# A rebuilt opening: packed small inputs, a moved silu, and filler matmuls on zeros, in a two-layer transformer kernel

## The chip, the cores and the metric

The kernel runs on one core of one Trainium2 chip. The metric is the device time of one execution in microseconds; the time before is 995.08 us, the median of 3 runs (993.34 to 995.79). Names of engines: PE is TensorE's matmul, PEld its weight load, DVE is VectorE, ACT is ScalarE, POOL is GpSimd, SP is SyncE, which only issues transfers here.

## The reference, cut to what matters

Two layers, 256 tokens, width 1024. Each layer has a feed-forward block, a mixer (sliding-window attention in layer 0, forgetting attention in layer 1) and a second feed-forward block. Every block is preceded by a modulated norm, whose shift, scale and gate come from the condition vector c.

```python
c_act = jax.nn.silu(c)
for layer in range(DEPTH):
    mod = (c_act @ ada_w[layer] + ada_b[layer]).reshape(B, 3, 3, D_MODEL)
    h = modulate(x, norm_g[layer, 0], mod[:, 0, 0], mod[:, 0, 1])
    x = x + 0.5 * mod[:, 0, 2][:, None, :] * swiglu(h, ffn_w13[layer, 0], ffn_w2[layer, 0])
    h = modulate(x, norm_g[layer, 1], mod[:, 1, 0], mod[:, 1, 1])
    ...
# modulate: rmsnorm(x, g) * (1 + scale) + shift
# swiglu:   gate, up = split(h @ w13); (silu(gate) * up) @ w2
```

All in float32, about 250 MB of weights read once.

## The kernel before

**A recorded program, then a list scheduler.** Everything in `_build` is only recorded: `Recorder.add` (line 185) notes each instruction with its tiles and an assumed duration, and `Recorder.run` (line 309) then plays the whole program against a model of the engines and emits the instructions in the order that comes out. PE takes its matmuls in the order of their place in the program (`at`), every other engine the ready instruction with the earliest due time, where `urgent` overrides the due time. Each engine afterwards executes its own list strictly in order. A different opening therefore shifts the model's clock, and can exchange neighbours far behind it. Nearly every instruction has line 238 in the profile, the line that emits it, so groups are told apart by their tiles.

**Precision by three matmuls.** A weight piece of 128 x 1024 float32 (512 KB) lands in `wraw`; ACT casts it to `whi`, DVE makes `wlo` = raw - hi; `mm3` multiplies hi by hi, hi by lo and lo by hi. Raw, hi, lo, activations (`hT`) and some others share one pool of 39 slots (tag "w").

**Modulation on DVE.** The rows of ada_w are not multiplied on PE. silu(c) is broadcast over 128 partitions as `cb`, and each piece of ada_w costs one DVE instruction over 1024 columns, a "dot" (SCALAR_TENSOR_TENSOR wraw<-wraw,cb), with the sum in one column of `mod`.

**The opening** (lines 504 to 552, `start` at 712). SP loads c (one row), x (two pieces), then by turns two pieces of ada and two of w13 (`w13s`). ACT's queue loads `colb` and `gcol`; POOL's queue loads `qkg`, `sink` and `bfb`, which are first used in later layers. ACT takes silu of c on one partition, PE broadcasts it with a row of ones, ACT copies it to `cb`. x is normalised (squares with a sum on ACT, `u` on DVE, the power -1/2 on POOL, `xn`), PE transposes it against `ident` and ACT copies the transposes to `xT`. Then come eight steps over k: two dots give column k of shift and scale, ACT makes h, `hT` hi and lo follow, and PE does 24 matmuls into eight accumulators ("pa" and "ps"), the first four chunks of the first feed-forward block. Afterwards these are gated (`sil`), transposed by PE and evacuated by ACT and DVE (`gT`), while ACT and DVE go on splitting weight pieces (w13a, w2).

**Later places that matter.** At about 70 us PE transposes `sil` of these first chunks and needs banks that the evacuation of `gT` frees; at about 188 us, the end of the first block, it needs the last `sil`, which stands in DVE's list among dots for the modulation of later blocks.

## Time and profile before

| what | before |
|---|---|
| median of 3 runs | 995.08 us (993.34 to 995.79) |
| the profiled execution | 994.5 us, span 992.7 us |
| PE busy | 972.6 us (98%), 4766 matmuls |
| DVE busy | 776.9 us (78%) |
| ACT busy | 528.2 us (53%) |
| transfers | 252.73 MB, mean 255 GB/s |

How to read it: the span goes from the first instruction to the last end; the execution's time is 1.8 us longer. A row of the timeline gives start, duration, engine, line, operation, tiles and shapes, and in brackets the idle time of the engine just before and what ended it. A row of the waits gives who waited for whom, the total in us, how often, and the longest. Windows give the busy time of each engine in a stretch, the granted clock, the busy share of the DMA engines and GB/s.

### The profile page before, as it was taken

What the parts mean: (1) busy time and instruction counts of PE and PEld (TensorE: products, weight loads), DVE (VectorE), ACT (ScalarE), POOL (GpSimd) and SP (SyncE); (2) the same over time, 40 slices, a digit from 0 to 9 for tenths busy, and PEclk for the clock granted to TensorE, in tenths of its full rate; (3) what the DMA queues carried; (4) which work ended last, traced back from release to release, by engine and by line L of the source; (5) the groups of instructions that cost most, each with busy time, mean ns of one, the idle gap of its engine ahead of it and who ended that gap; (6) DMA issues with size and microseconds to landing.
All of it is one profiled execution on the core that took longest, in us unless ns stands there. A gap on an engine that the chain in (4) does not pass through costs nothing.

```text
span 992.7 us, 13662 instructions
## 1 busy us (share of the span) xinstructions
PE 972.6 (98%) x4766; PEld 816.3 (82%) x4766; DVE 776.9 (78%) x1396; ACT 528.2 (53%) x946; POOL 48.2 (5%) x73
## 2 busy tenths in 40 slices
PE   6999999999999999999999999999999999999998
PEld 4878788798888888888888888889899888888886
DVE  5999989985899988767898788658788998554622
ACT  6583434465986454444554453437677776444420
POOL 1000000012100000000100000001221010000000
PEclk9999999999999999999999999999999999999999
DMA  9999999856347987776788879744437458656501
GB/s 338 409 390 383 402 361 409 307 172 215 129 156 252 337 334 285 291 294 233 275 317 304 312 279 352 247 157 161 139 112 266 161 197 282 224 198 220 211 8 64
DMA packets 74247, 252.73 MB, mean 255 GB/s; under 512 B 8497, under 2 KB 11969, under 8 KB 74178
## 3 DMA queue, kind: packets, MB, share of 16 engines
q1 hardware_dynamic: 73186, 249.63, 68.6%
q10 hardware_dynamic: 896, 2.21, 0.6%
q8 instruction: 37, 0.61, 0.2%
q0 software_dynamic: 96, 0.02, 0.2%
q14 instruction: 32, 0.26, 0.1%
HBM read 249.95 MB, written 1.88 MB: 254 GB/s over the span
## 4 chain that ended last, share of the span: by engine, by line
PE 91%; DVE 4%; ACT 2%; DMA 2%; issue 1%; POOL 0%; SPq 0%; DVEq 0%; POOLq 0%
PE ps L238 57%; PE pa L238 34%; DVE wraw L238 1%; DVE wlo L238 1%; DMA wraw<-in_w13s 1%; DMA M<-foxsc 1%; ACT t L238 1%; POOL qrs L238 0%; ACT PT L238 0%; DVE t L238 0%; DVE gT L238 0%; DVE sil L238 0%; ACT whi L238 0%; SPq L238 0%; DVE qss L238 0%
## 5 line engine op out<-in xcount | busy, mean ns | idle before, releaser
L238 PE MATMUL ps<-whi,hT 128*128 128x512 f32 (+2 forms) x1728 | 534.8, 382 | 0.0
L238 ACT CAST whi<-wraw 128x1024 fp32r<-128x1024 f32 (+2 forms) x328 | 329.5, 1024 | 218.6 <-DMA wraw<-in_w 72.4
L238 DVE TENSOR_TENSOR wlo<-wraw,whi 128x1024 fp32r<-128x1024 f32 (+2 forms) x328 | 381.3, 1180 | 67.0 <-ACT whi L238 49.2
L238 PEld LDWEIGHTS ps<-whi,hT 128*128 128x128 f32 x1728 | 321.5, 188 | 52.9 <-issue 0.6
L238 PE MATMUL ps<-wlo,hT 128*128 128x512 f32 (+2 forms) x864 | 328.1, 381 | 0.0
L238 PE MATMUL pa<-whi,gT 128*128 128x512 f32 x704 | 218.0, 391 | 0.0
L238 DVE SCALAR_TENSOR_TENSOR wraw<-wraw,cb 128x1024 f32<-128x1024 f32 x144 | 173.3, 1218 | 15.5 <-DMA wraw<-in_ada 15.1
L238 PEld LDWEIGHTS ps<-wlo,hT 128*128 128x128 f32 x864 | 162.4, 188 | 26.1 <-issue 0.2
L238 PEld LDWEIGHTS pa<-whi,gT 128*128 128x128 f32 x704 | 131.9, 188 | 27.2
L238 PE MATMUL pa<-wlo,gT 128*128 128x512 f32 x352 | 133.3, 390 | 0.0
L238 ACT ACTIVATE sil<-ps 128x256 f32<-128x256 f32 x84 | 32.0, 384 | 105.6 <-PE ps L238 105.4
L238 PEld LDWEIGHTS pa<-wlo,gT 128*128 128x128 f32 x352 | 66.1, 188 | 13.6
L238 DVE TENSOR_TENSOR sil<-sil,ps 128x256 f32<-128x256 f32 x84 | 34.6, 414 | 48.2 <-ACT sil L238 48.1
L238 DVE TENSOR_TENSOR gT<-ps,gT 128x256 fp32r<-128x256 f32 x88 | 33.5, 415 | 8.9 <-ACT gT L238 8.9
L238 PE MATMUL pa<-whi,OT 128*128 128x512 f32 x128 | 39.1, 393 | 0.0
L238 PE MATMUL pa<-PT,zeroed 128*128 128x256 f32 (+1 forms) x192 | 36.3, 287 | 0.5 <-DVE PT L238 0.4
L238 ACT ACTIVATE t<-x 128x512 f32<-128x512 f32 x24 | 15.0, 625 | 40.8 <-DVE x L238 38.9
L238 DVE SCALAR_TENSOR_TENSOR t<-gate,pa 128x512 f32<-128x512 f32 (+1 forms) x26 | 15.6, 640 | 25.6 <-DMA gate<-gsc 12.9
L238 ACT CAST gT<-ps 128x256 fp32r<-128x256 f32 x88 | 29.1, 378 | 12.2 <-PE ps L238 11.6
L238 PEld LDWEIGHTS pa<-PT,zeroed 128*128 128x128 f32 x192 | 30.1, 191 | 3.8 <-DVE PT L238 1.2
L238 POOL TENSOR_TENSOR qrs<-qss,mhalf 128x4 f32<-128x4 f32 (+1 forms) x24 | 26.8, 1118 | 87.3 <-DVE qss L238 86.3
L238 PE MATMUL ps<-ident,sil 128*128 128x128 f32 x176 | 27.9, 272 | 2.6 <-DVE sil L238 1.4
(113 smaller groups left out, 650.7 us busy)
## 6 DMA issues: line engine op xcount, KB each, us to landing
wraw<-in_ada SPq DMA_DIRECT2D x144, 512.0 KB, 7.5
wraw<-in_w13b SPq DMA_DIRECT2D x132, 512.0 KB, 6.3
wraw<-in_w SPq DMA_DIRECT2D x88, 512.0 KB, 5.6
wraw<-in_w13a SPq DMA_DIRECT2D x28, 512.0 KB, 10.2
wraw<-in_fwin SPq DMA_DIRECT2D x28, 384.0 KB, 3.8
wraw<-in_w13s SPq DMA_DIRECT2D x16, 512.0 KB, 10.2
wraw<-in_swin SPq DMA_DIRECT2D x16, 384.0 KB, 5.2
wraw<-in_swout SPq DMA_DIRECT2D x8, 512.0 KB, 3.7
```

What stands on the lines that cost most here:

```text
L238: return lambda: getattr(real, method)(*[un(v) for v in a], **{n: un(v) for n, v in k.items()})
```

## The change

Five small inputs become one array of 232 columns that one transfer on ACT's queue brings; qkg, sink and bfb are now slices of it, and POOL issues no transfers. silu moves from the row of c to the copies after the broadcast; a silu of one column (`tb`) comes first on ACT, so that the table load is at the start. 21 matmuls of 128 x 512 on a zeroed tile `wz` are recorded as fillers: the model gives one to PE whenever nothing else is ready for it there, and they end up at fixed places in PE's list. Their results are never read. Three of the four squares of the first norm go to DVE (the model may choose, by `also`), all four `xn` run on DVE, and h in `start` is fixed on ACT. The second half of x's transposes (`transposed_x(1)`) stands behind the first chunk of the first step.

```diff
+NWARM = 21
...
-        pes = sorted((o for o in ops if o.eng == "PE"), key=lambda o: o.at)
+        pes = sorted((o for o in ops if o.eng == "PE" and not o.filler), key=lambda o: o.at)
+        fillers = [o for o in ops if o.filler]
...
+                    if pick is None and e == "PE" and fillers and fillers[0].wait == 0 and t >= fillers[0].ready:
+
+                        o = fillers.pop(0)
+                        busy[e] = t + o.dur * (2 if cold else 1)
+                        active += busy[e] - t
+                        heapq.heappush(events, busy[e])
+                        finish(o, t, busy[e])
+                        continue
...
+    ones = cp.tile([P, P], F32, name="ones")
+    G.memset(ones, 1.0)
+    warm = psum()
+    wz = wp.tile([P, 512], F32R, tag="w", name="wz")
+    G.memset(wz.bitcast(F32), 0.0)
+    rec.filler = True
+    for _ in range(NWARM):
+        T.matmul(warm, wz[:, 0:P], wz, start=True, stop=True)
+    rec.filler = False
+    rec.urgent = -70e3
+    tb = cp.tile([P, 1], F32, name="tb")
+    A.activation(tb, ones[:, 0:1], AF.Silu)
...
-    colb = cp.tile([P, 2, 9, KT], F32, name="colb")
-    A.dma_start(colb, ap["colb"])
+    small = cp.tile([P, 232], F32, name="small")
+    A.dma_start(small, ap["small"])
+    colb = small[:, 0:144].rearrange("p (l s k) -> p l s k", l=2, s=9)
+    gcol = small[:, 144:192].rearrange("p (s k) -> p s k", s=6)
+    qkg = small[:, 192:196].rearrange("p (a b) -> p a b", a=2)
+    sink = small[:, 196:212]
+    bfb = small[:, 212:228]
     colb1 = cp.tile([P, 2, 3, KT], F32, name="colb1")
-    gcol = cp.tile([P, 6, KT], F32, name="gcol")
-    A.dma_start(gcol, ap["gcol"])
...
-    A.activation(crow, crow, AF.Silu)
     cb = cp.tile([P, D], F32, name="cb")
     for i in range(2):
         pc = psum()
         T.matmul(pc, ones[0:1, :], crow[:, i * 512 : i * 512 + 512], start=True, stop=True)
-        A.copy(cb[:, i * 512 : i * 512 + 512], pc)
+        A.activation(cb[:, i * 512 : i * 512 + 512], pc, AF.Silu)
...
-        G.dma_start(qkg, ap["qkg"])
         V.tensor_scalar(out=qkg[:, :, 0], in0=qkg[:, :, 0], scalar1=HD ** -0.5, scalar2=None, op0=ALU.mult)
-        G.dma_start(sink, ap["sink"].to_broadcast([P, NH]))
         V.tensor_scalar(out=msink, in0=sink, scalar1=-1.0, scalar2=None, op0=ALU.mult)
-        G.dma_start(bfb, ap["bf"].to_broadcast([P, NH]))
...
-            A.activation(t, x[h][:, c], AF.Square, scale=1.0 / 32.0, accum_out=ss[:, dh : dh + 1])
+            o = A.activation(t, x[h][:, c], AF.Square, scale=1.0 / 32.0, accum_out=ss[:, dh : dh + 1])
+            if first:
+                rec.also(o, V, "scalar_tensor_tensor", out=t, in0=x[h][:, c], scalar=1.0 / 1024.0, in1=x[h][:, c],
+                         op0=ALU.mult, op1=ALU.mult, accum_out=ss[:, dh : dh + 1])
...
-        xn = [norm(0), norm(1, A)]
+        rs = [rstd(h, True) for h in range(2)]
         xT = []
-        for g in range(2):
+
+        def transposed_x(g):
             t = wp.tile([P, 4, S], F32, tag="w", name="xT")
             for h in range(2):
+                xn = bp.tile([P, 512], F32, tag="b", name="xn")
+                V.tensor_scalar(out=xn, in0=x[h][:, g * 512 : g * 512 + 512], scalar1=rs[h], scalar2=None, op0=ALU.mult)
                 pt = psum()
...
+        transposed_x(0)
...
+            A.activation(t, xT[k // 4][:, k % 4, :], AF.Identity, scale=mod[1][:, k : k + 1], bias=mod[0][:, k : k + 1])
...
+                if k == 0 and c == 1:
+                    transposed_x(1)
```

**Where instructions move: the opening.** PE's list before, from its start to the first main matmuls (`gate,ones` is the broadcast of c, `ident,xn` the transposes of x):

```order
L238 MATMUL ps<-gate,ones 128x512 x2
L238 MATMUL ps<-ident,xn 128x128 x16
L238 MATMUL pa<-whi,hT_214 128x512
L238 MATMUL pa<-wlo,hT_214 128x512
L238 MATMUL pa<-whi,hT_214 128x512
```

PE's list now:

```order
L240 MATMUL ps<-wz 128x512 x4
L240 MATMUL ps<-gate,ones 128x512 x2
L240 MATMUL ps<-wz 128x512 x9
L240 MATMUL ps<-ident,xn 128x128 x4
L240 MATMUL ps<-wz 128x512 x2
L240 MATMUL ps<-ident,xn 128x128 x4
L240 MATMUL ps<-wz 128x512 x6
L240 MATMUL pa<-whi,hT_211 128x512
L240 MATMUL pa<-wlo,hT_211 128x512
L240 MATMUL pa<-whi,hT_211 128x512
L240 MATMUL pa<-wlo,hT_211 128x512
L240 MATMUL pa<-whi,hT_222 128x512 x2
```

Fillers stand around the broadcast and between the transposes; the other eight transposes follow after six main matmuls. ACT's list before, up to its first h:

```order
L238 ACTIVATE gate<-gate 1x1024
L238 ACTIVATE t,ss<-x_94 128x512
L238 ACTIVATE t,ss<-x_99 128x512 x2
L238 COPY cb<-ps 128x512
L238 ACTIVATE t,ss<-x_94 128x512
L238 ACTIVATE xn<-x_99,rs 128x512
L238 COPY cb<-ps 128x512
L238 CAST whi<-wraw 128x1024
L238 COPY xT<-ps 128x4x128 x2
L238 ACTIVATE xn<-x_99,rs 128x512
L238 CAST whi<-wraw 128x1024
L238 ACTIVATE h_206<-xT,mod_183,mod_170 128x256
```

and now:

```order
L240 ACTIVATE tb<-ones 128x1
L240 ACTIVATE t,ss<-x_90 128x512
L240 ACTIVATE cb<-ps 128x512 x2
L240 COPY xT<-ps 128x4x128
L240 CAST whi<-wraw 128x1024
L240 COPY xT<-ps 128x4x128
L240 ACTIVATE h_209<-xT,mod_194,mod_180 128x256
```

One square and the silus of cb remain ahead of the first cast, and one weight cast instead of two stands ahead of h.

**At about 70 us**, ACT, from the gating of the first chunks to the evacuation of their transposes (`gT`). Before:

```order
L238 ACTIVATE sil<-pa 128x256 x2
L238 CAST whi<-wraw 128x1024
L238 ACTIVATE sil<-pa 128x256 x2
L238 CAST whi<-wraw 128x1024
L238 ACTIVATE sil<-ps 128x256 x4
L238 CAST whi<-wraw 128x1024 x6
L238 CAST gT<-ps 128x2x128 x7
```

and now:

```order
L240 ACTIVATE sil<-pa 128x256 x2
L240 CAST whi<-wraw 128x1024
L240 ACTIVATE sil<-pa 128x256 x2
L240 CAST whi<-wraw 128x1024
L240 ACTIVATE sil<-ps 128x256 x2
L240 CAST whi<-wraw 128x1024
L240 ACTIVATE sil<-ps 128x256 x2
L240 CAST whi<-wraw 128x1024 x5
L240 CAST gT<-ps 128x2x128 x8
```

Before, the first cast of this row is the first w2 piece and eight w2 casts precede gT; now the first is the last piece of w13a, and seven w2 casts precede it.

**At about 188 us**, DVE, around the last two `sil` of the block (the rows with `wraw,mod` are dots). Before:

```order
L238 SCALAR_TENSOR_TENSOR wraw,mod_1670<-wraw,cb 128x1024
L238 TENSOR_TENSOR sil<-sil,ps 128x256
L238 TENSOR_TENSOR gT<-ps,gT 128x2x128 x2
L238 SCALAR_TENSOR_TENSOR wraw,mod_1670<-wraw,cb 128x1024 x4
L238 TENSOR_TENSOR sil<-sil,ps 128x256
L238 TENSOR_TENSOR gT<-ps,gT 128x2x128
L238 SCALAR_TENSOR_TENSOR wraw,mod_1670<-wraw,cb 128x1024
```

and now:

```order
L240 TENSOR_TENSOR sil<-sil,ps 128x256
L240 TENSOR_TENSOR gT<-ps,gT 128x2x128 x2
L240 SCALAR_TENSOR_TENSOR wraw,mod_1692<-wraw,cb 128x1024 x3
L240 TENSOR_TENSOR sil<-sil,ps 128x256
L240 TENSOR_TENSOR gT<-ps,gT 128x2x128
L240 SCALAR_TENSOR_TENSOR wraw,mod_1692<-wraw,cb 128x1024
L240 TENSOR_TENSOR gT<-ps,gT 128x2x128
```

One dot fewer stands ahead of each of the two, so that two dots fewer precede the last `sil` in all, with as many weight splits (66 `wlo`) as before. Behind the residual that follows, the lists of all engines are the same as before, and on PE they differ outside the opening only by a few exchanged neighbours.

More of the change, by code (lines that the diff above doesn't have):

```diff
@@ L167 @@
     __slots__ = ("eng", "emit", "dur", "deps", "succ", "bases", "due", "n", "wait", "ready", "start", "end",
-                 "bytes", "at", "bg", "urgent", "alts", "paced", "port", "part", "group", "table")
+                 "bytes", "at", "bg", "urgent", "alts", "paced", "port", "part", "group", "table", "filler")
 class Engine:
@@ L182, in __init__ @@
         self.bg, self.urgent, self.paced, self.marks, self.group = False, None, None, [], None
+        self.filler = False
     def add(self, eng, real, method, a, k):
@@ L354, in run @@
         low, group, last, table = 0, None, None, None
-        pes = sorted((o for o in ops if o.eng == "PE"), key=lambda o: o.at)
+        pes = sorted((o for o in ops if o.eng == "PE" and not o.filler), key=lambda o: o.at)
+        fillers = [o for o in ops if o.filler]
         for o in ops:
             o.wait, o.ready = len(o.deps), 0.0
-            if not o.wait:
+            if not o.wait and not o.filler:
                 heapq.heappush(pending, (0.0, o.n))
@@ L376, in finish @@
                 s.ready = max(s.ready, o.end + lat(o, s))
-                if not s.wait:
+                if not s.wait and not s.filler:
                     heapq.heappush(pending, (s.ready, s.n))
@@ L527, in _build @@
                     channel_multiplier=1)
-    ones = cp.tile([P, P], F32, name="ones")
-    G.memset(ones, 1.0)
     rec.urgent = -60e3
-    A.activation(crow, crow, AF.Silu)
     cb = cp.tile([P, D], F32, name="cb")
@@ L539, in _build @@
                     scalar1=1.0, scalar2=None, op0=ALU.add)
-    qkg = cp.tile([P, 2, 2], F32, name="qkg")
-    sink = cp.tile([P, NH], F32, name="sink")
     msink = cp.tile([P, NH], F32, name="msink")
-    bfb = cp.tile([P, NH], F32, name="bfb")
     def small_inputs():
-        G.dma_start(qkg, ap["qkg"])
         V.tensor_scalar(out=qkg[:, :, 0], in0=qkg[:, :, 0], scalar1=HD ** -0.5, scalar2=None, op0=ALU.mult)
-        G.dma_start(sink, ap["sink"].to_broadcast([P, NH]))
         V.tensor_scalar(out=msink, in0=sink, scalar1=-1.0, scalar2=None, op0=ALU.mult)
-        G.dma_start(bfb, ap["bf"].to_broadcast([P, NH]))
     def load(src):
@@ L664, in residual, with rstd @@
                 yield c
-    def rstd(h):
+    def rstd(h, first=False):
         ss = tp.tile([P, 2], F32, tag="ss", name="ss")
@@ L676, in rstd, with norm @@
         return rs
-    def norm(h, eng=None):
+    def norm(h):
         rs = rstd(h)
@@ L683, in norm @@
             t = bp.tile([P, 512], F32, tag="b", name="xn")
-            if eng is A:
-                A.activation(t, x[h][:, c], AF.Copy, scale=rs)
-            else:
-                V.tensor_scalar(out=t, in0=x[h][:, c], scalar1=rs, scalar2=None, op0=ALU.mult)
+            V.tensor_scalar(out=t, in0=x[h][:, c], scalar1=rs, scalar2=None, op0=ALU.mult)
             xn.append(t)
@@ L731, in modulated @@
             t = sp.tile([P, S], F32, tag="s", name="h0")
-            o = V.tensor_scalar(out=t, in0=xT[k // 4][:, k % 4, :], scalar1=mod[1][:, k : k + 1],
-                                scalar2=mod[0][:, k : k + 1], op0=ALU.mult, op1=ALU.add)
-            rec.also(o, A, "activation", t, xT[k // 4][:, k % 4, :], AF.Identity, scale=mod[1][:, k : k + 1],
-                     bias=mod[0][:, k : k + 1])
+            A.activation(t, xT[k // 4][:, k % 4, :], AF.Identity, scale=mod[1][:, k : k + 1], bias=mod[0][:, k : k + 1])
             hi, lo = hTk(hT, k, slice(0, S))
@@ L1233, in _layout @@
     col = lambda v: np.concatenate([v, v])
-    a["qkg"] = np.stack([np.stack([col(f["swa_q_g"][0]), col(f["swa_k_g"][0])], 1),
+    qkg = np.stack([np.stack([col(f["swa_q_g"][0]), col(f["swa_k_g"][0])], 1),
                          np.stack([col(f["fox_q_g"][0]), col(f["fox_k_g"][0])], 1)], 1)
-    a["sink"] = f["swa_sink"].reshape(1, NH)
-    a["bf"] = f["fox_b_f"].reshape(1, NH)
+    row = lambda v: np.broadcast_to(v.reshape(1, NH), (P, NH))
+    a["small"] = np.concatenate([a.pop("colb").reshape(P, -1), a.pop("gcol").reshape(P, -1), qkg.reshape(P, -1),
+                                 row(f["swa_sink"]), row(f["fox_b_f"]), np.zeros((P, 4), np.float32)], axis=1)
     onehot = np.zeros((32, 384), np.float32)
```

4 lines of the change are left out of this document (2 added, 2 removed).

## The prediction

> **What bounds the kernel now.** I read the busy shares first, then the waits of TensorE (PE), then the opening's timeline, then the two later places where PE waits.
>
> ```profile
> PE 972.6 (98%) x4766; PEld 816.3 (82%) x4766; DVE 776.9 (78%) x1396; ACT 528.2 (53%) x946; POOL 48.2 (5%) x73
> ```
>
> ```profile
> PE ps L238 <- ACT xn L238: 5.1, 2, 3.2
> PE ps L238 <- ACT gate L238: 4.1, 1, 4.1
> PE ps L238 <- DVE gT L238: 2.1, 2, 1.2
> ...
> PE ps L238 <- DVE sil L238: 1.4, 1, 1.4
> ```
>
> The second view is PE's waits over the whole span (total us, times, longest). PE works 972.6 of 992.7 us, and 9.2 us of its idle time lie in the opening. So PE sets the end: a microsecond by which its main work starts earlier is one off the time, unless PE meets a later wait whose cause has not moved. The opening as PE has it:
>
> ```profile
> 2.93 1.05 ACT L238 ACTIVATE gate<-gate 1x1024 f32<-1x1024 f32 x1
> ...
> 4.13 3.74 PE L238 MATMUL ps<-gate,ones 1*128 1x512 f32 x4 [4.13 <-ACT gate L238]
> ...
> 15.09 1.97 PE L238 MATMUL ps<-ident,xn 128*128 128x128 f32 x8 [3.24 <-ACT xn L238]
> ...
> 16.95 0.80 PE L238 MATMUL pa<-whi,hT 128*128 128x512 f32 x1
> ...
> 17.55 0.63 PE L238 MATMUL pa<-wlo,hT 128*128 128x512 f32 x1
> ...
> 17.97 0.63 PE L238 MATMUL pa<-whi,hT 128*128 128x512 f32 x1
> ```
>
> and two pieces of the chain of waits (start, us, what):
>
> ```profile
> 17.06 4.54 PE pa L238 x12
> ...
> 24.33 2.72 PE pa L238 x12
> ```
>
> The main matmuls start at 16.95; the first twelve take 4.54 us, the next dozen into the same accumulators 2.72. Start to start is 0.42 at first (17.55 to 17.97) and 0.23 later (2.72/12): the array starts at about half speed, which costs 1.8 us here, a stall included. The granted clock of the windows says 1.00 all along, so the spacing has to be read.
>
> What the first main matmul waits for, in order of time:
>
> ```profile
> 9.54 0.57 ACT L238 COPY cb<-ps 128x512 f32<-128x512 f32 x1
> ...
> 12.40 1.05 ACT L238 CAST whi<-wraw 128x1024 fp32r<-128x1024 f32 x1 [2.28 <-DMA wraw<-in_w13s]
> ...
> 13.41 0.15 DVE L238 TENSOR_TENSOR mod<-mod,colb 128x1 f32<-128x1 f32 x1
> ...
> 15.86 0.60 ACT L238 ACTIVATE h<-xT,mod,mod 128x256 f32<-128x256 f32 x1
> ...
> 16.50 0.40 ACT L238 CAST hT<-h 128x256 fp32r<-128x256 f32 x1
> ```
>
> What the DMA engines moved meanwhile (windows of 1 us: PE, PEld, DVE, ACT and POOL busy, clock, DMA share, GB/s; last the queue's row of the page):
>
> ```profile
> 5.00:6.00 1.00, 1.00 (x3) 0.36 (x2) 0.00 (x0) 0.60 (x2) 0.00 (x0) 1.00 1.05 289
> 6.00:7.00 1.00, 1.00 (x3) 0.30 (x1) 0.17 (x1) 0.40 (x1) 0.00 (x0) 1.00 1.48 295
> 7.00:8.00 1.00, 0.87 (x2) 0.00 (x0) 0.03 (x1) 1.00 (x5) 0.00 (x0) 1.00 0.77 30
> 8.00:9.00 1.00, 0.00 (x0) 0.00 (x0) 0.19 (x1) 1.00 (x4) 0.57 (x1) 1.00 0.69 247
> 9.00:10.00 1.00, 0.30 (x2) 0.31 (x3) 0.29 (x2) 1.00 (x3) 0.40 (x1) 1.00 1.01 411
> ...
> q0 software_dynamic: 96, 0.02, 0.2%
> ```
>
> The DMA engines were busy from 5 to 9 us and delivered 289, 295, 30 and 247 GB/s instead of 411: missing are 122+116+381+164 = 783 KB, or 1.9 us at 411. The only traffic of that stretch that isn't a big load is POOL's queue, q0: the three small transfers qkg, sink and bfb, 0.02 MB that took 0.2% of sixteen engines' span, 2.0 us. The first weight piece came at 12.4.
>
> **The change, part by part.**
>
> *Packed small inputs.* Five transfers become one on ACT's queue; its rows of 928 B replace rows of 576 and 192 B, so what ACT's queue moves stays about the same (116 KB after 96). POOL's three go. Bounds for what that gives the load stream: 0 (if the big loads would have stalled anyway) to 1.9 us. I take 1.9, since the two accounts, the missing bytes and the share of q0, agree. Every later load then lands 1.9 us earlier as long as the stream is full, which it is, at about 410 GB/s, until the first slot waits near 70 us.
>
> The Trainium skill's page "DMA: Bandwidth & Descriptors", in its section on the anatomy of one DMA, gives a POOL-issued transfer a fixed time of about 2.0 us plus its bytes at 436 GB/s. By that, 18 KB take 0.04 us of bandwidth, the rest is latency that other queues could use, and this term would be near 0: that is the first rival below.
>
> *silu behind the broadcast.* The 1.05 us silu on one row goes away; PE broadcasts c itself, and the two copies of cb become silus of the same size (0.57). With four fillers ahead (from 1.6 when wz is zeroed, 0.42 each; c itself is there by 2.93) the broadcast runs 3.3 to 7.0, and cb is complete at 7.6 rather than at 10.1, because ACT has one square ahead of it and not four squares and an xn. Cover: DVE is not ready for the first dot by then.
>
> *Squares and xn on DVE, h on ACT.* DVE now has three of the four squares and all four xn, in place of two xn; they lie in its idle time before the first dot. h already ran on ACT. Rows for the durations:
>
> ```profile
> L238 DVE SCALAR_TENSOR_TENSOR t<-gate,pa 128x512 f32<-128x512 f32 (+1 forms) x26 | 15.6, 640 | 25.6 <-DMA gate<-gsc 12.9
> ```
>
> ```profile
> 3.50 0.33 POOL L238 MEMSET cmask<- 128x256 f32 x1
> ...
> 6.61 0.63 ACT L238 ACTIVATE t<-x 128x512 f32<-128x512 f32 x1 [1.01 <-DMA x<-in_x]
> ...
> 8.27 0.57 POOL L238 TENSOR_TENSOR rs<-u,mhalf 128x1 f32<-128x1 f32 x1 [4.08 <-DVE u L238]
> ...
> 10.19 0.49 DVE L238 TENSOR_SCALAR xn<-x,rs 128x512 f32<-128x512 f32 x1 [0.67 <-POOL rs L238]
> ```
>
> (The 512-column memset of wz is taken as twice cmask's.) The second half of x lands at 6.6; two squares of 0.64, u 0.2, rs 0.57 with two hops 0.8, xn 0.5: first dot at 9.4, two dots of 1.15 to 11.7, mods ready at 12.0, 1.5 us earlier than before (13.41 and 0.15). ACT meanwhile: first weight piece at 10.5, whi to 11.5, second copy of xT (the size of cb's, 0.57) to 12.1, h to 12.7, hT to 13.1. So **the main matmuls could start at 13.2** in place of 16.95.
>
> *Fillers.* They stand in PE's queue ahead of the transposes, so they can be late themselves. After the broadcast (7.0): nine fillers, four transposes, two, four, six. All at half speed (0.42; a transpose 1.97/8 = 0.25) they end at 16.1; all at twice that they would end at 11.6, and the start stays 13.2. Before, full speed came some 3.5 us after matmuls of this width began to follow each other; from 7.0 that is 10.5, and then the nine end at 10.7, the second transposes at 12.2, xT's copy behind whi at 13.4, hT at 14.4: start at 14.45, 2.5 us earlier. I take this middle value; bounds 16.1 and 13.2. The first step then runs at full speed (+1.8), but eight transposes of g = 1 now stand inside it (8 x 0.12 = 1.0, cover gone). **PE is 2.5 + 1.8 - 1.0 = 3.3 us early** when it enters the second step; bounds -1.1 (all slow: 0.85, no 1.8, transposes 1.97) and 4.6 (3.75 + 0.8).
>
> On that clock the Trainium skill's page "TensorE: Matmul & The Clock Gate", Part 1, says that full speed follows one busy window of about 3.4 us, and that the window runs freely. By it the four fillers and the broadcast would already count and the start would be 13.2; the broadcast's 3.74 us before, which by this rule might have raised the clock, are followed by slow transposes, but 11 us later, so no row here decides it. The sum below comes out the same with either start.
>
> *Later places.*
>
> ```profile
> 17.48 1.22 DVE L238 SCALAR_TENSOR_TENSOR wraw<-wraw,cb 128x1024 f32<-128x1024 f32 x1
> ...
> 22.64 1.22 DVE L238 SCALAR_TENSOR_TENSOR wraw<-wraw,cb 128x1024 f32<-128x1024 f32 x1
> ```
>
> Steps of the opening cost PE 5.44 us (2 x 2.72) and DVE less (its dots start at 17.48 and 22.64: 5.16), so supply keeps ahead. Then:
>
> ```profile
> 55.99 1.05 ACT L238 CAST whi<-wraw 128x1024 fp32r<-128x1024 f32 x1 [0.18 <-DMA wraw<-in_w13a]
> ...
> 62.77 5.79 ACT L238 CAST whi<-wraw 128x1024 fp32r<-128x1024 f32 x6
> ...
> 70.59 0.44 PE L238 MATMUL ps<-ident,sil 128*128 128x128 f32 x2 [1.21 <-DVE gT L238]
> ...
> 105.74 1.05 ACT L238 CAST whi<-wraw 128x1024 fp32r<-128x1024 f32 x1 [4.14 <-PE ps L238]
> ...
> 134.98 1.05 ACT L238 CAST whi<-wraw 128x1024 fp32r<-128x1024 f32 x1 [4.86 <-DMA wraw<-in_w13a]
> ...
> 183.08 1.21 DVE L238 SCALAR_TENSOR_TENSOR wraw<-wraw,cb 128x1024 f32<-128x1024 f32 x1
> ...
> 187.66 0.41 DVE L238 TENSOR_TENSOR sil<-sil,ps 128x256 f32<-128x256 f32 x1
> ...
> 188.13 0.44 PE L238 MATMUL ps<-ident,sil 128*128 128x128 f32 x2 [1.39 <-DVE sil L238]
> ```
>
> At 70 us PE waits for gT, which ACT makes after eight w2 casts; in the new order after seven. The seventh piece lands seven landings after 55.97, at 1.28 us each (512 KB at 410 GB/s) and two tiny transfers between, 65.2; cast, two evacuations, PE at 67.2, less 1.9: 65.3. PE itself arrives at 69.4 - 3.3 = 66.1. So the wait goes and **PE is 4.5 early**. The other of the two waits for gT (2.1 - 1.2 = 0.9) is near 109, behind a cast that waits 4.14 for PE's own slots: that moves with PE.
>
> At 188 PE waits for sil, and DVE has four dots on end ahead of it (183.08 to 187.66). This is the narrow place. The new order has two dots fewer ahead of that sil: 2 x 1.15 = 2.3 us. Beyond this the sil comes earlier only as DVE's whole stream does, and that stream waited for loads at 134.98. With loads 1.9 us earlier the limit is 2.3 + 1.9 = 4.2; PE could use 4.5 + 1.39. **The sum: 4.2 us**, the smaller of the two. The two dots come later, ahead of the residual, where DVE idled 1.63 for PE. From here on the orders are the same, and a shift of PE stays.
>
> The profiled execution took 994.5 (span 992.7 and 1.8 around it), 0.6 under the median of the three runs, 995.08. 994.5 - 4.2 = 990.3 for the like execution, and 995.08 - 4.2 = **990.9** for the median.
>
> **Rivals.** What a measurement here can tell from no change is about 0.3%, 3.0 us.
>
> 1. *The small transfers cost nothing.* Loads land as before; DVE's stream does not move, and the limit at 188 is 2.3: 992.8. For it: 0.02 MB is little. Against it: the 30 GB/s window. The Trainium skill's fit ("DMA: Bandwidth & Descriptors", as above) would side with this rival.
> 2. *The fillers do not raise the clock*, as the broadcast did not. PE enters the second step 1.1 late, gets 1.21 back at 70 and 1.39 at 188, since supply is early: 1.5 gained, 993.6. Against it: the fillers fill all 128 rows, the broadcast one.
> 3. *The packed transfer lands late, and it is slower.* All of DVE's work now stands behind it (its first instruction makes colb1 from it). First dot = landing + 4.2 (0.64 for three small ones, 3.6 as above), so from 6.4 us on it costs. Were it served behind the eight loads of SP's queue (8 x 1.28 + 2.7 = 12.9), the first dot comes at 17.1, PE starts 3.8 later (as 13.2 after 9.4), at 20.9, 4.0 late, 3.2 after the faster first step, and gets only the 1.2 of 70 us back, since DVE's stream is late too: 997.1. It decides from a landing at 10.9 on, and passes 0.3% from 13.9. Against it: colb alone landed ahead of x.
>
> ```profile
> 2.67 0.30 DVE L238 TENSOR_SCALAR colb<-colb 128x48 f32<-128x48 f32 x1 [2.67 <-DMA colb<-in_colb]
> ```
>
> **How the numbers follow.** Forecast 0.62, rival 1 0.18, rival 2 0.10, rival 3 0.06; 0.04 for a re-sorted order between 60 and 190 us that meets another wait. Within the forecast the gain runs from 2.5 (loads gain half) to 5.9 (DVE's stream follows PE's slots wholly), of which nine tenths pass 3.0: faster by over 0.3% 0.60 with a fifth of rival 1; within it 0.35, with most of rivals 1 and 2 and half of rival 3; slower 0.05. The range is 988.9 to 994.0: below 5.9 us of gain and some scatter, above rivals 1 and 2.
>
> **What would show it.** No dip to 30 GB/s between 5 and 9 us and the first w13s piece near 10.5; cb complete by 7.6; the first main matmuls 0.23 apart, starting between 13.2 and 16; PE's wait near 66 gone; a wait for sil near 184 still there, and longer than 1.39, as the sign that DVE's order and the loads set the gain. It is wrong if PE enters the second step less than 2 us early, if that last wait swallows more than PE brings, or if whi waits longer for loads in the first 70 us.

## The result, and the profile after

The changed kernel takes 989.83 us in the median of 6 runs (989.33 to 991.01), the kernel before 995.24 in the median of its 6 (993.31 to 996.18); the ratio is 0.9949, with a 95% interval of 0.9939 to 0.9959. That is 5.4 us less. The profiled execution took 991.01 us, with a span of 989.2.

The waits of PE over the whole span, of the changed kernel (us in total, times, longest):

```profile
PE ps L240 <- POOL wz L240: 1.5, 1, 1.5
PE pa L240 <- DVE qn L240: 1.2, 2, 1.0
PE ps L240 <- DVE sil L240: 0.9, 1, 0.9
PE pa L240 <- ACT hT L240: 0.9, 1, 0.9
PE ps L240 <- DVE gT L240: 0.4, 1, 0.4
```

The 9.2 us that PE idled in the opening have become 2.4 (wz and hT), because fillers now lie there; the two waits for gT (2.1) have shrunk to one of 0.4, and the wait for the last sil from 1.4 to 0.9. The opening as PE, SP, ACT and DVE have it (rows of the timeline):

```profile
3.46 3.78 PE L240 MATMUL ps<-gate,ones 1*128 1x512 f32 x4
7.17 4.10 PE L240 MATMUL ps<-wz 128*128 128x512 f32 x9
11.11 0.60 PE L240 MATMUL ps<-ident,xn 128*128 128x128 f32 x4
...
14.89 0.50 PE L240 MATMUL pa<-whi,hT 128*128 128x512 f32 x1 [0.88 <-ACT hT L240]
15.23 0.39 PE L240 MATMUL pa<-wlo,hT 128*128 128x512 f32 x1
15.46 0.40 PE L240 MATMUL pa<-whi,hT 128*128 128x512 f32 x1
...
10.40 1.61 SPq L240 DMA_DIRECT2D wraw<-in_w13s  x2
...
11.75 0.59 ACT L240 COPY xT<-ps 128x512 f32<-128x512 f32 x1 [3.87 <-PE ps L240]
12.23 1.05 ACT L240 CAST whi<-wraw 128x1024 fp32r<-128x1024 f32 x1
...
15.83 1.23 DVE L240 TENSOR_TENSOR wlo<-wraw,whi 128x1024 fp32r<-128x1024 f32 x1
```

The main matmuls start at 14.89 (16.95 before) and follow each other by 0.23 us at once. The first w13s piece has landed at 10.38 (12.37 before; SP issues the next pair right behind that landing, here at 10.40). But its cast starts at 12.23, against 12.40 before: in ACT's list it stands behind the copy of xT, that copy waits for the transposes, and these stand behind nine fillers, which ran at half speed until the ninth (4.10 us for nine). And so DVE's second weight split starts at 15.83, hardly earlier than before:

```profile
16.00 1.22 DVE L238 TENSOR_TENSOR wlo<-wraw,whi 128x1024 fp32r<-128x1024 f32 x1 [1.30 <-ACT whi L238]
...
214.65 1.03 PE L238 MATMUL ps<-ident,xn 128*128 128x128 f32 x8
```

(This is the kernel before.) Its second row is the yardstick of all that follows: the transposes of a later norm, behind all places that the change touches. In the changed kernel the same eight transposes start 5.17 us earlier, and the places on the way are these (PE at 67 us, DVE's last sil, PE behind it, and PE at the yardstick):

```profile
67.11 0.44 PE L240 MATMUL ps<-ident,sil 128*128 128x128 f32 x2 [0.43 <-DVE gT L240]
...
182.32 0.41 DVE L240 TENSOR_TENSOR sil<-sil,ps 128x256 f32<-128x256 f32 x1
...
182.79 0.44 PE L240 MATMUL ps<-ident,sil 128*128 128x128 f32 x2 [0.89 <-DVE sil L240]
...
209.48 1.09 PE L240 MATMUL ps<-ident,xn 128*128 128x128 f32 x8
```

I call **lead** how much earlier the n-th matmul (fillers not counted) starts than in the kernel before, read from the two traces. The lead of the changed kernel is 2.8 us at 24 us, when the first step is over; 3.5 behind the place at 70 us; 4.55 behind the one at 108 us, where the wait is gone; 5.1 behind the one at 182 us (188 before); and it stays so until 265 us. So half of the gain is the opening, and half comes from three places behind it.

On the times: in some executions of most of these kernels the granted clock falls to about a half for some microseconds between 255 and 280 us, which costs 1 to 8 us there (2.1 in the profile above), so that I compare leads at the yardstick and take the times only as their intervals allow.

### The profile page after: what moved, and what is told of

Its sections match the earlier page's. It is cut to its first block, busy times and chain, and to the rows that moved or that the text cites. A ratio compares the mean times of both kernels' runs of the same rounds, so it can differ in the third digit from the quotient of the medians.

```text
span 989.2 us, 13698 instructions
## 1 busy us (share of the span) xinstructions
PE 978.8 (99%) x4787; PEld 822.0 (83%) x4787; DVE 779.2 (79%) x1404; ACT 523.9 (53%) x938; POOL 47.2 (5%) x71
## 4 chain that ended last, share of the span: by engine, by line
PE 93%; DVE 3%; ACT 2%; issue 1%; DMA 1%; POOL 0%; DVEq 0%; POOLq 0%
PE ps L240 59%; PE pa L240 35%; DVE wlo L240 1%; DVE wraw L240 1%; DMA M<-foxsc 1%; ACT t L240 1%; POOL qrs L240 0%; ACT whi L240 0%; DVE t L240 0%; ACT PT L240 0%; ACT sil L240 0%; DVE sil L240 0%; DVE qss L240 0%; DVE gT L240 0%; DVE qn L240 0%
## 5 line engine op out<-in xcount | busy, mean ns | idle before, releaser
L240 PEld LDWEIGHTS pa<-wlo,gT 128*128 128x128 f32 x352 | 66.1, 188 | 13.7
L240 PE MATMUL pa<-PT,zeroed 128*128 128x256 f32 (+1 forms) x192 | 38.4, 302 | 0.3 <-DVE PT L240 0.2
L240 PEld LDWEIGHTS pa<-PT,zeroed 128*128 128x128 f32 x192 | 32.4, 205 | 3.3 <-DVE PT L240 0.9
L240 ACT ACTIVATE t<-t,nm 128x129 f32<-128x129 f32 (+3 forms) x64 | 28.9, 454 | 1.7 <-DVE nm L240 1.5
```

Source lines behind the costliest of these rows:

```text
L240: return lambda: getattr(real, method)(*[un(v) for v in a], **{n: un(v) for n, v in k.items()})
```

## The experiments

All runs in one table. The lead at 24 us is what the opening gave; the next three columns are what was added to it at the three places (rounded, they add up to within 0.2); the lead at the yardstick is the difference of its row to 214.65. Cast and split are the start of the first weight cast and of the second weight split, in us. The last two columns are the median time of the kernel, with that of the kernel before measured beside it, and the ratio of the two.

| kernel | cast | split | lead at 24 | at 70 | at 108 | at 182 | yardstick | median us (before) | ratio, 95% interval |
|---|---|---|---|---|---|---|---|---|---|
| before | 12.40 | 16.00 | 0 | 0 | 0 | 0 | 0 | | |
| changed | 12.23 | 15.83 | 2.8 | 0.7 | 1.05 | 0.5 | 5.17 | 989.83 (995.24) | 0.9949, 0.9939 to 0.9959 |
| changed, again (e11) | 12.30 | 15.89 | 2.75 | 0.7 | 1.05 | 0.2 | 4.79 | 991.7 (995.62) | 0.9967, 0.9943 to 0.9991 |
| fillers off (e1) | 10.93 | 14.64 | 1.7 | 0.75 | 1.05 | 1.3 | 4.87 | 990.4 (995.71) | 0.9963, 0.9946 to 0.9981 |
| opening, old lists (e2) | 12.75 | 16.35 | 2.3 | -3.2 | 0.9 | -0.5 | -0.53 | 995.7 (995.71) | 1.0014, 0.9987 to 1.0040 |
| old opening, new lists (e3) | 11.87 | 15.47 | 1.3 | 0.8 | 1.05 | 0.5 | 3.74 | 993.2 (995.71) | 0.9981, 0.9958 to 1.0004 |
| packed inputs alone (e4) | 10.37 | 14.15 | 1.8 | 0 | 0 | 0 | 1.82 | 993.56 (995.71) | 0.9980, 0.9966 to 0.9995 |
| pool transfers back (e5) | 12.01 | 15.60 | 3.0 | 0.7 | 1.05 | 1.5 | 6.27 | 989.0 (994.63) | 0.9937, 0.9914 to 0.9960 |
| two dots back (e6) | 12.74 | 16.34 | 2.3 | 0.7 | 1.05 | -3.7 | 0.44 | 995.15 (994.63) | 0.9995, 0.9980 to 1.0011 |
| one dot behind (e7) | 12.44 | 16.03 | 2.6 | 0.7 | 1.05 | 0.0 | 4.37 | 990.28 (994.63) | 0.9956, 0.9940 to 0.9971 |
| fillers behind transposes (e8) | 11.21 | 14.93 | 3.7 | 0.7 | 1.05 | 0.15 | 5.72 | 989.61 (994.63) | 0.9936, 0.9912 to 0.9961 |
| the same again (e10) | 10.33 | 14.06 | 4.6 | 0.7 | 1.05 | 1.0 | 7.43 | 988.48 (995.62) | 0.9932, 0.9906 to 0.9957 |
| packed, new lists (e9) | 10.01 | 13.93 | 2.6 | 0.8 | 1.05 | 0.85 | 5.40 | 995.39 (995.62) | 0.9978, 0.9958 to 0.9999 |
| e10 with pool transfers (e12) | 12.13 | 15.72 | 2.9 | 0.65 | 1.05 | 1.5 | 6.14 | 988.67 (995.39) | 0.9925, 0.9898 to 0.9952 |

Each lead compares one execution with one execution of the kernel before, and the same opening did not always give the same lead. The six kernels with the changed opening's order (changed, e11, e2, e5, e6 and e7) lead by 2.3 to 3.0 us at 24 us, the less the later full speed came: the traces record the full clock from 10.51 us on in e5 (lead 3.0), from 11.02 and 11.18 in the two executions of the changed kernel (2.8 and 2.75), 11.47 in e7 (2.6), 12.66 in e6 and 13.21 in e2 (2.3 each). So half a microsecond between two single profiles is no result, and the columns for the three places say more than the yardstick.

Where an order was to be kept or put together, the kernel got a table in place of the scheduler's result, and nothing else was changed in the instructions:

```diff
         done.sort(key=lambda o: o.start)
+        at, done = 0, []
+        for step in struct.unpack(f'<{len(self.ops)}h', zlib.decompress(base64.b85decode(ORDER))):
+            at += step
+            done.append(self.ops[at])
```

### Which part of the change brings the gain (e1 to e4)

**e1: the changed kernel without its fillers.** Their results were never read; all else keeps its place.

```diff
-            o.emit()
+            if not o.filler:
+                o.emit()
```

> The changed kernel with every list as it is, but the 21 filler matmuls are not issued. Theory S (the lists and the loads set the gain: at about 182 us PE waits for a sil that DVE brings when its own list lets it, and whatever PE brings beyond that is lost there): PE starts near 13.2 but at half speed, enters the second step near 22.4 instead of 21.4, about 1.0 later, and still leaves the place at 182 us at the same time, so the time is that of the changed kernel, 989.8 within 0.4. Theory P (PE's early, full-speed start is the gain and every later wait moves with it): 1.0 is lost for good, 990.8.

**e2: the changed opening, and behind it the orders of the kernel before; e3: the reverse**, both by the table above.

> The changed opening, but from the last step of the opening on every engine's list is in the order of the kernel before (one weight split more ahead of gT at 70 us, two more ahead of gT near 108, two dots more ahead of the last sil at 188). Theory S: those places hold PE back as before: about 2.8 gained over before (5.1 less the two dots' 2.3), near 992.3. Theory P: the order is a side effect, 5.1 gained, near 989.9.

> The kernel before, opening and all, with the lists of the changed kernel from the last step of the opening on. Nothing of the opening's work is changed. Theory S: PE gets back the waits at 70 (1.2), 108 (0.9) and 188 (1.4) as far as the two dots allow, 2.3 us: 992.8. Theory P: nothing, 995.1.

**e4: the kernel before with the packed transfer alone**, in its own order.

```diff
-    A.dma_start(colb, ap["colb"])
-    A.dma_start(gcol, ap["gcol"])
-        G.dma_start(qkg, ap["qkg"])
-        G.dma_start(sink, ap["sink"].to_broadcast([P, NH]))
-        G.dma_start(bfb, ap["bf"].to_broadcast([P, NH]))
+    A.dma_start(small, ap["small"])
```

> The kernel before with the five small inputs packed into one transfer and all lists as before. Theory S and the prediction: no dip in the loads between 6 and 8 us, the first weight piece near 10.5, PE's main matmuls near 15.3, and 1.9 gained at 188: 993.2. Rival 1 of the prediction (the small transfers cost nothing): 995.1, first piece still at 12.4.

e1, PE and ACT in the opening:

```profile
10.93 1.04 ACT L240 CAST whi<-wraw 128x1024 fp32r<-128x1024 f32 x1
...
13.64 0.79 PE L240 MATMUL pa<-whi,hT 128*128 128x512 f32 x1 [2.51 <-ACT hT L240]
14.23 0.63 PE L240 MATMUL pa<-wlo,hT 128*128 128x512 f32 x1
14.66 0.63 PE L240 MATMUL pa<-whi,hT 128*128 128x512 f32 x1
```

Without fillers the main matmuls start 1.25 us *earlier* (13.64 against 14.89) but 0.43 apart, at half speed; the lead at 24 us is 1.1 us less. So the fillers do raise the clock, and they delay the start by what they hold up. At the yardstick only 0.3 us of it are left, 4.87 against 5.17, less than one execution of the changed kernel differs from the next (4.79 in e11).

e3, PE at the last sil and at the yardstick, then e4, the first cast and the yardstick:

```profile
184.20 0.44 PE L242 MATMUL ps<-ident,sil 128*128 128x128 f32 x2 [0.86 <-DVE sil L242]
...
210.91 1.09 PE L242 MATMUL ps<-ident,xn 128*128 128x128 f32 x8
```

```profile
10.37 1.05 ACT L242 CAST whi<-wraw 128x1024 fp32r<-128x1024 f32 x1 [0.47 <-DMA wraw<-in_w13s]
...
212.83 1.04 PE L242 MATMUL ps<-ident,xn 128*128 128x128 f32 x8
```

e3 has the new lists only, and its places at 70, 108 and 182 add the same 0.8, 1.05 and 0.5 as in the changed kernel: 2.35 in all, as theory S had it (2.3). (Its lead of 1.3 at 24 us is none of the lists': its opening is that of before, but in that execution the loads came 0.5 us earlier and the full clock is recorded from 18.33 us on instead of 20.45.) Its median of 993.2 us alone would not show it; the interval reaches 1.0004. e4 has the packed inputs only: the cast follows the landing at once, the lead is 1.8 at 24 us, and with the old lists the three places add nothing; it stays 1.82 to the yardstick, as theory S said.

e2 was expected to gain 3 us by S, or 5 by P, and gained nothing. Its PE rows:

```profile
65.55 1.69 PE L244 MATMUL ps<-ident,sil 128*128 128x128 f32 x14
69.88 0.44 PE L244 MATMUL ps<-ident,sil 128*128 128x128 f32 x2 [2.64 <-DVE gT L244]
...
72.95 1.05 PE L244 MATMUL ps<-whi,hT 128*128 128x512 f32 x2
73.81 0.63 PE L244 MATMUL ps<-wlo,hT 128*128 128x512 f32 x1
```

and its windows (busy time of PE, PEld, DVE, ACT and POOL, granted clock, DMA share, GB/s):

```profile
66.00:70.00 4.00, 1.36 (x13) 1.12 (x12) 4.00 (x6) 3.23 (x10) 0.00 (x0) 1.00 1.00 389
70.00:74.00 4.00, 4.00 (x13) 3.12 (x14) 3.96 (x11) 1.42 (x2) 0.00 (x0) 0.65 0.61 198
```

PE arrives 2.2 us earlier at the place at 70 us, where DVE's old list has seven splits from 60 us on ahead of gT (the new one five), and DVE itself is no earlier than before (second split at 16.35). PE waits 2.64 us instead of 1.21, and then the array runs at half speed (two matmuls in the 0.86 us from 72.95 to 73.81; granted clock 0.65 in that window). The wait takes 1.4 us of the lead and the slow stretch another 1.6: the lead falls from 2.15 to -0.9. So an early start of PE alone is worth less than nothing if neither DVE's start nor its list moves with it; in e4, where the second split is 1.85 us earlier, the lead of 1.8 passes all three places untouched. Neither theory had that.

### What the loads are worth, and what the dots are worth (e5 to e8)

**e5: the changed kernel with qkg, sink and bfb in transfers of their own again**, on POOL's queue; all orders are kept, and so is the packed transfer on ACT's queue (the text below counts four such transfers, the kernel has three).

```diff
+        G.dma_start(qkg, ap["qkg"])
+        G.dma_start(sink, ap["sink"].to_broadcast([P, NH]))
+        G.dma_start(bfb, ap["bf"].to_broadcast([P, NH]))
```

> The changed kernel with every engine's order kept, but the four small inputs again in transfers of their own, three of them on POOL's queue. Theory L (the prediction's term: the loads' 1.9 us are worth 1.9 us at the place near 182 us): the first w13s piece lands at 12.3 instead of 10.4, TensorE's advance over the kernel before falls from 5.1 us (changed kernel, at 200 us) to 3.2 us, time 1.9 us above the changed kernel's, some 991.7 us. Theory D (VectorE's list, which begins with the first weight split and has 0.8 us of idle time until 66 us, sets it; that split waits in the changed kernel for ScalarE's cast at 12.23 us, behind the fillers, however early the weights are): the cast moves by 0.2 to 0.5 us, the advance stays 4.6 to 5.0 us, time 990.0 to 990.4 us.

**e6 and e7: dots moved in DVE's list around the last sil** (two to ahead of it, or one to behind it):

```diff
 e6                                        e7
 SCALAR_TENSOR_TENSOR wraw<-wraw,cb x3      SCALAR_TENSOR_TENSOR wraw<-wraw,cb x2
+SCALAR_TENSOR_TENSOR wraw<-wraw,cb x2      TENSOR_TENSOR sil<-sil,ps
 TENSOR_TENSOR sil<-sil,ps                  TENSOR_TENSOR gT<-ps,gT
 TENSOR_TENSOR gT<-ps,gT                   +SCALAR_TENSOR_TENSOR wraw<-wraw,cb
```

> The changed kernel with two of VectorE's dots moved back ahead of the last sil product (five instead of three between the gT before it and it), nothing else moved. Theory S (VectorE's list ahead of that sil sets TensorE's restart near 182 us): TensorE's wait there grows from 0.89 to 3.2 us, its advance over the kernel before falls from 5.1 to 2.8 us, time 2.3 us above the changed kernel's, some 992.1 us. Theory P (TensorE's early start is the gain): no change, 989.8 us.

> The changed kernel with one more dot moved behind that sil product and the gT after it (two instead of three ahead). Theory S: the sil product is ready 1.14 us earlier, TensorE's wait of 0.89 us near 182 us is gone, the advance grows from 5.1 to 6.0 us, time 988.9 us. Against it, theory B (buffers): the dot also gives its weight buffer free 1.5 us later, the stream of w_in pieces behind it starts late by as much, and TensorE waits for those between 184 and 200 us: advance 4.5 to 5.1 us at 200 us, time 989.8 us or more.

**e8: the fillers moved in PE's list**; the last four are left out.

```diff
 MATMUL ps<-gate,ones x4
-MATMUL ps<-wz x9
+MATMUL ps<-wz x3
 MATMUL ps<-ident,xn x4
 MATMUL ps<-wz x2
 MATMUL ps<-ident,xn x4
-MATMUL ps<-wz x6
+MATMUL ps<-wz x8
```

> The changed kernel with three instead of nine wide fillers between the broadcast and the first transposes, two between the transposes as before, eight behind them, and the last four left out (no result uses them). Both theories: transposes at 8.5 instead of 11.1 us, the first weight cast at 10.4 instead of 12.23, the first main matmul at 13.0 to 13.5 instead of 14.89 at full speed. Theory D (VectorE's list from its first split on): VectorE is 1.0 to 1.5 us earlier until 66 us, its releases pull the weight stream forward with it, and the advance after 188 us grows from 5.1 to 6.1 to 6.6 us: 988.3 to 988.8 us. Theory L (the stream is set by when its first transfers start, which does not move): the weights land when they did, the advance after 188 us stays 5.1 us, 989.8 us.

e5, ACT's first cast and PE's yardstick in the timeline, and a window of the weight stream:

```profile
12.01 1.05 ACT L244 CAST whi<-wraw 128x1024 fp32r<-128x1024 f32 x1
...
208.38 1.09 PE L244 MATMUL ps<-ident,xn 128*128 128x128 f32 x8
```

```profile
140.00:160.00 20.00, 20.00 (x91) 16.54 (x90) 18.97 (x29) 9.48 (x13) 0.00 (x0) 1.00 1.03 418
```

The first w13s piece landed at 11.96, 1.6 us later than in the changed kernel, and it cost nothing: the cast starts at 12.01, the lead at 24 us is 3.0, and at 101 us the weights land when the changed kernel's do (the 71st piece at 100.93 and 100.90). Theory L, the prediction's term, falls. That e5 leads even by 6.27 at the yardstick is another matter: from there on its pieces come ahead of the changed kernel's, by 1.3 us at 116, 1.8 at 131 and 2.3 at 182, so that the sil there is ready before PE comes. The speed of the stream, 418 GB/s where the changed kernel's ran at 409 in the same window, is worth 1.1 us over forty pieces, but 1.8 were there ahead of that window, most of it in two jumps that are not explained. (e11, the changed kernel once more, has jumps of 0.3 to 1.0 us against the first profile of the same program, in both directions.)

e6, PE in the timeline, and a window behind the wait (the granted clock is the 0.50):

```profile
185.92 0.44 PE L244 MATMUL ps<-ident,sil 128*128 128x128 f32 x2 [3.51 <-DVE sil L244]
```

```profile
188.00:190.00 2.00, 2.00 (x7) 1.52 (x6) 2.00 (x4) 1.66 (x3) 0.00 (x0) 0.50 0.83 323
```

The wait grows from 0.89 to 3.51 us, 2.6 against the 2.3 expected; and as in e2 the clock falls to 0.50 behind it, which costs 1.6 us more. Two dots in the wrong place thus take 4.2 us at this place (3.7 lost where the changed kernel gains 0.5), most of the gain of the change; the other 0.5 that e6 lacks at the yardstick is its opening, with the full clock 1.6 us later. e7, PE:

```profile
182.49 0.44 PE L244 MATMUL ps<-ident,sil 128*128 128x128 f32 x2 [0.34 <-DVE sil L244]
...
198.84 1.06 PE L244 MATMUL ps<-ident,xn 128*128 128x128 f32 x8 [0.92 <-DVE xn L244]
```

One dot less ahead of the sil takes 0.55 us off that wait and makes one of 0.92 at 198 us, for the xn of the next norm, which stands behind the same dot in DVE's list. Nothing is gained (4.37). Theory S falls for this step and so does the reason of B: it isn't the weights that come late, it is DVE's own work. In all kernels DVE has done 73 splits and 64 dots when it comes to that xn; the order only moves PE's wait about.

e8 has its second split at 14.93 instead of the 14.1 expected, since in that execution the first weights landed 0.8 us later than in the changed kernel's profile; the lead at 24 us was 3.7, the yardstick's 5.72. That is below D's 6.1 and above L's 5.1, and so decides nothing alone.

### The two that were left to separate (e9 to e12)

**e9: the kernel before with the packed inputs and the new lists, and nothing else of the change. e10: e8 once more. e11: the changed kernel once more.**

> The kernel before with two things alone: the packed small inputs, and the changed kernel's order behind the opening (no fillers, silu ahead of the broadcast and h where they were). Theory A (what counts is VectorE's list and when it starts; the packed inputs start it 1.8 us earlier where ScalarE's first cast is free, as in the run with the packed inputs alone, and the lists are worth 3.7 us as in the run with the old opening): second weight split at 14.2 us, TensorE's advance over the kernel before 1.8 us at 24 us and 5.2 to 5.5 us at 200 us, time 989.3 to 989.9 us where the kernel before has 994.6, as good as the whole change. Theory R (the rest of the opening is needed): advance at 200 us 3.7 to 4.0 us, 991 us.

> The kernel with the fillers behind the transposes once more, unchanged. In its first profile the first w13s piece had landed at 11.19 us, 0.8 us later than in the changed kernel's profile (10.38), for no reason in the program. Theory D (VectorE's start decides): where it lands at 10.4 us, the first cast follows at 10.4, the second split at 14.1 instead of 14.93, and TensorE's advance at 200 us is 6.2 to 6.5 us, time 988.0 to 988.5 us at 994.6 of the kernel before. Against it: an advance of 5.6 us again, 989.0 us, with the waits near 182 us as in the first run, set by the weight stream.

> The changed kernel itself, as the yardstick for the two others on the same chip and for how far one profile of it differs from the next. All theories: advance at 200 us within 0.6 us of 5.1, time 5 us below the kernel before.

**e12: e10 with the three transfers on POOL's queue again**, by the edits of e5 and e8.

> The kernel with the fillers behind the transposes, and with it the three transfers on POOL's queue again, as in the run with the pool transfers back. Theory C (the loads' 1.9 us count only where ScalarE's first cast stands ready for them: there, with the cast held by the fillers until 12.2 us, they cost nothing; here the cast has followed the landing at 10.3): the first w13s piece lands at 11.9 to 12.4, the first cast with it, the second weight split goes from 14.1 to 15.6 to 16.0 us, TensorE's advance over the kernel before at 200 us falls from 7.4 to 5.3 to 6.0 us, time 1.5 to 2 us above that of the fillers behind the transposes. Theory N (the pool transfers cost nothing anywhere, as the run with them back would have it): second split at 14.1 to 14.5, advance 6.5 to 7.4 us.

e9's yardstick, then e10's opening and yardstick, then e11's and e12's:

```profile
209.25 1.09 PE L242 MATMUL ps<-ident,xn 128*128 128x128 f32 x8
```

```profile
10.33 1.04 ACT L244 CAST whi<-wraw 128x1024 fp32r<-128x1024 f32 x1
...
13.13 0.50 PE L244 MATMUL pa<-whi,hT 128*128 128x512 f32 x1
13.46 0.40 PE L244 MATMUL pa<-wlo,hT 128*128 128x512 f32 x1
...
14.06 1.23 DVE L244 TENSOR_TENSOR wlo<-wraw,whi 128x1024 fp32r<-128x1024 f32 x1
...
207.22 1.09 PE L244 MATMUL ps<-ident,xn 128*128 128x128 f32 x8
```

```profile
11.44 1.61 SPq L240 DMA_DIRECT2D wraw<-in_w13s  x2
...
12.30 1.05 ACT L240 CAST whi<-wraw 128x1024 fp32r<-128x1024 f32 x1
```

```profile
12.13 1.05 ACT L244 CAST whi<-wraw 128x1024 fp32r<-128x1024 f32 x1 [1.83 <-DMA wraw<-in_w13s]
...
208.51 1.09 PE L244 MATMUL ps<-ident,xn 128*128 128x128 f32 x8
```

e9 leads by 5.40, as theory A said: at the yardstick the packed inputs and the lists alone are worth as much as the whole change, which has 5.17 and 4.79. The parts are not A's, though: 2.6 instead of 1.8 at 24 us, for the full clock is recorded from 17.28 us on where e4 has it from 18.75, and 2.7 instead of 3.7 from the lists. And its time does not show the gain: the median is 995.39, and in the profile the clock's fall near 260 us takes 6.4 us of the lead (5.15 at 265 us, -1.3 at 280). e10 shows what the rest is worth when it isn't in its own way: with three fillers ahead of the transposes and eight behind, the cast starts at 10.33, the main matmuls at 13.13 and at full speed, and the lead is 7.43, more than theory D's 6.5. It is the version that beats both kernels, by the two profiles 2.3 us ahead of the changed one (0.55 in e8); in times the intervals of e8 and e10 still overlap with that of the changed kernel.

e11 shows the same as e5 without any edit: the first w13s piece landed 1.05 us later than in the first profile of the same program (SP's next pair at 11.44 against 10.40), and the cast came 0.07 later. e12 is the counterpart: with the cast freed, the late loads hold it until 12.13, the second split comes at 15.72 instead of 14.06 and the lead at 24 us is 2.9 instead of 4.6. Theory C holds there. Of these 1.65 us 0.35 are got back by the yardstick, at the place at 182 us, where this kernel, like e5, has its weights early (0.5 us ahead of e10's, after being 1.5 behind at 101 us); 6.14 at the yardstick lies between the two theories, nearer to C's 5.3 to 6.0. The medians, 988.67 and 988.48 us, do not show the 1.5 to 2 us of theory C.

Put together, of the 5.2 us of the changed kernel the new lists give 2.25 to 2.35 (e3), and the opening 2.8. In the opening, full speed from the fillers is 1.1 (e1), of which 0.3 arrive at the yardstick; the packed transfer, though worth 1.8 alone (e4), adds nothing measurable here (e5).

## Why the prediction was right, and where it was not

The time, the sign and the range were right: 990.9 foretold, 989.83 measured. The sum of 4.2 came out as 5.2, for partly other reasons, and it is partly luck that it came so near.

- **Loads 1.9 us earlier: right as a landing, wrong as a term.** The dip is gone (377, 414, 422 and 422 GB/s in the windows from 5 to 9 us), and the first w13s piece came 1.99 us earlier in the profile (a dip of its own, 246 and 238 GB/s from 5 to 7 us, makes it 0.94 in e11). The engines were not busy all through the old dip, as the prediction has it: their share was 0.77 and 0.69 from 7 to 9 us. But the sum added 1.9 at the last sil, and e5, e11 and e12 show that in this kernel the loads wait for the cast, not the cast for the loads. The step that failed is the order on ACT: I put the first cast at 10.5, at the landing, ahead of the copy of xT; it stands behind one, which waits for the fillers. (The 13.4 that the prediction gives for xT's copy behind whi fits only a cast near 11.8, so the sum for the start already had the cast late, while the full 1.9 was kept for DVE.) Only 0.17 us of the 1.99 reached DVE. Where the cast is free the term has its size (e4: 1.8; e10 to e12: 1.65).
- **On rival 1** the landings decide against it: three transfers of 0.02 MB moved the next loads by 1.6 to 2.0 us here. With them on POOL's queue the first w13s piece lands at 11.84 to 12.37 (before, e3, e5, e12), without them at 9.98 to 11.43 (the ten others). The fixed-time fit of the Trainium skill ("DMA: Bandwidth & Descriptors", anatomy of one DMA), by which the term would be near 0, does not give what such transfers take from another queue. Yet its effect, that nothing is gained by them in this kernel, is what e5 measured.
- **Start of the main matmuls: right within the bounds.** 14.89 for 14.45, and by the mechanism given (fillers at half speed, transposes behind them). Full speed came between the ninth filler's start, 10.75, and the transposes at 11.11 (the trace records the full clock from 11.02 on), 3.6 to 3.9 us after the wide fillers begin at 7.17; I had taken 3.5. (The 11 us between the old broadcast and the transposes are from start to start; from its end they are 7.2.)
- **2.5 + 1.8 - 1.0 = 3.3 early in the second step: 2.8.** The start came 0.44 later than taken, which is most of it.
- **At 70 us: a wait left, not none.** PE resumed at 67.1 and not at 66.1. I computed the seventh landing; what ends last there is DVE, whose five splits run on end until 66.72 ahead of gT. Added: 0.7 instead of 1.2.
- **Near 109: wrong.** I let the wait of 0.9 move with PE. It is gone, in e3 too, where only the lists are new (1.05 in each run with them): two splits and a cast fewer stand ahead of that gT.
- **At 188: the narrow place was the right one, and the two dots the right cause** (e6: 2.6 us of wait for 2.3). The sil came 5.3 us earlier rather than 4.2. Of this 2.3 are the dots; 1.0 is a wait of DVE for a cast at 160.9 us, gone in the new order; the remaining 2 are the weight stream, ahead by 2.0 us there. I had given that to the early loads; e5 contradicts it, and which of the reordered splits and dots freed the buffers sooner wasn't separated. That its size is near the 1.9 of the sum is luck; in e11 the stream is 1.2 ahead at that place. e3 adds up in the same way: its sil comes 3.9 earlier, with the dots' 2.3, the wait's 1.0 and a stream 0.6 ahead. The sign that I named, a wait longer than 1.39, did not come (0.89).
- **Rival 2** fell: the main matmuls are 0.23 apart in the changed kernel and 0.43 in e1. **Rival 3** did not occur: DVE's first instruction has the packed array at 2.84 us. **The chances** put 0.04 on lists that meet another wait; e2 and e6 show how near that was: some 5 and 4 us by the order of a handful of instructions.

The experiments' own theories: S (lists and loads) was right on the lists and wrong on the loads; P (PE's early start is carried on) holds for the opening's 2.8, but only where DVE's list or its start lets it pass, as e2 and e4 show side by side.

## What to carry to other kernels

Work that is put ahead of a path to prepare it (here fillers for the clock) also stands in that path's queue: follow what waits behind it, through every engine's list, down to the first instruction of the engine that sets the pace. A scheduler that is given a changed opening hands out another order far behind it; test the opening and the order apart before either gets the credit. And a term such as "loads 1.9 us earlier" counts only up to the first instruction that wasn't waiting for them.
